# Summing a modulation column two blocks after its load, writing residuals eight products later, and running attention head 0 ahead of delta-rule head 0

## The chip, the cores and the metric

The kernel runs as one program on one core of a Trainium2 chip. The metric is the device time of one execution in microseconds (us); three executions of the kernel before gave a median of 1952.88 us. The core has a matrix engine (TensorE, called PE in the profile; its weight loads are PEld), a vector engine (VectorE, DVE), a scalar engine (ScalarE, ACT), a general engine (GpSimd, POOL), and a sync engine (SyncE, SP), which here issues all DMAs.

## The reference

One decoder layer on 256 rows of width 2048, all in float32:

```
mod = silu(c) @ ada_w + ada_b            # 9 vectors of 2048: sh1 sc1 gt1 sh2 sc2 gt2 sh3 sc3 gt3
h = ada_in(x, norm_g[0], sh1, sc1)       # rmsnorm(x)*(1+scale)+shift
x = x + 0.5 * gt1 * swiglu(h, ...)       # first feed-forward, inner width 5632
h = ada_in(x, norm_g[1], sh2, sc2)
x = x + gt2 * hybrid_mixer(h, ...)       # 8 attention heads with a forget gate (fox), 8 gated delta-rule heads (gdn)
h = ada_in(x, norm_g[2], sh3, sc3)
x = x + 0.5 * gt3 * swiglu(h, ...)       # second feed-forward
return rmsnorm(x, final_norm)
```

## The kernel before, in words

**Products in two parts.** PE multiplies float32 data as a rounded high part plus a low part. Every weight is therefore split on the core. The weights come as 674 blocks of eight 128x128 tiles, in the order in which PE uses them. `Stream.block` issues the DMA of a block on SP (`wraw`, L119) and rounds it on ACT to the high part (`whi`, L121); `Stream.next` subtracts on DVE to get the low part (`wlo`, L133). Each of the three tiles has a pool of four buffers (the raw blocks have one more during the feed-forwards), so SP loads block n when DVE has done `wlo` of block n-4, and DVE can be up to four blocks ahead of PE. In what follows a place is named by block number: blocks 1 to 264 are the first feed-forward, 265 to 378 the mixer's input projections with the heads woven in, 379 to 410 its output projection, 411 to 674 the second feed-forward.

**Modulation columns.** `mod` is computed in 144 columns of 128 values. `ada_col` loads 1 MB of weights for one column (`adat`, L253, on SP right behind a weight load) and then one DVE instruction multiplies and sums it (`total`, L257). The table `RATE` says how many columns are due per block from a given block on (0.1 from block 264, 0.25 from 280, 0.125 from 408). From the mixer on `W.late` is set, and a column's sum is not recorded at its load but put into `W.owing`; the next call of `Stream.next` that opens a block calls `settle`, which records all owed sums. `ada_need`, called before a residual or a norm uses a column, also settles all.

**Mixer.** `ORDER` lists the steps: K, G, V, Z and F project a column group of a head; G starts the delta-rule chain of a head (`gdn`), F the attention chain (`fox`). Chains are generators: between products, `tick` advances a clock by 0.35 per product and lets a chain record its next piece when the number that it yielded has passed. `finish` records all that is left of a chain at once. The chain `solve` inverts 16x16 blocks for four heads: it writes them to DRAM (`ld`, L951), reads them back, does 15 pairs of DVE instructions (L964, L965), writes the result to DRAM (`lt`, L970), reads it back (L974) and multiplies (L977). Step G of head 0 calls `finish("k", 3)`, which needs `solve` of the first four heads.

**Residuals.** After the last product of an output tile, `residual` adds the PSUM tile to `x` with two DVE instructions (L506, L507; L504 before them halves the gate).

**What sets the order.** The code records instructions; the layer that builds the program then orders each engine's queue by the place of recording and by what it estimates to be ready, unless `issue_after` ties an instruction behind another one of its engine. Each engine works through its queue in that order, and an instruction that waits holds up all behind it on that engine.

Of the kernel before, what the change touches and what calls it, by code (L numbers as in the profile page):

```python
# [8 lines left out]
F32 = mybir.dt.float32  # L9
# [4 lines left out]
ALU = mybir.AluOpType  # L14
# [5 lines left out]
KD = D // P  # L20
# [8 lines left out]
WB = 8  # L29
# [3 lines left out]

RATE = ((0, 0.5), (24, 0.34), (56, 0.45), (68, 0.06), (112, 0.5), (168, 0.38), (264, 0.1), (280, 0.25), (408, 0.125))
N_BIG, N_GDN = 3, 3
# [4 lines left out]
HIDX = 3  # L40
MORE = True

HA = 128 + 16
# [4 lines left out]
GAP = {"k": 1.0, "gdn": 1.0, "fox": 1.2, "out": 1.0}  # L48
ORDER = ("K3 K4 K5 K6 K7 Z0 V0 G0 F0 G1 F1 G2 F2 G3 F3 V1 Z1 G4 F4 G5 F5 G6 G7 F6 F7").split()
N_O = 17  # L50
# [38 lines left out]
class Stream:  # L89
# [11 lines left out]

    def settle(self):

        while self.owing:
            self.owing.pop(0)()

# [17 lines left out]
    def next(self, mat, k, n, width=1):  # L124
        i = len(self.order)
        if i % WB == 0:
            nc = self.nc
            b = i // WB
            r, lo = self.first.pop(0) if self.first else self.block(b)
            self.l = lo.tile([P, WB * P], F32R, name="wlo")  # L130
            pace = [r_ for r_ in RATE if r_[0] <= b][-1][1]
            with self.behind():
                nc.vector.tensor_tensor(self.l, r, self.h.bitcast(F32), ALU.subtract)  # L133
            self.settle()
            self.owed += 0.0 if self.quiet else pace
            while self.owed >= 1.0:
                self.owed -= 1.0
                self.side()
# [8 lines left out]
def layer_kernel(ctx: ExitStack, tc: tile.TileContext, xrow, c, adaw, cols, cst, w, out, order, dbg=None):  # L147
# [86 lines left out]
    def ada_col():  # L234
# [20 lines left out]
        def total():  # L255
            with W.behind(False):
                V.tensor_tensor_reduce(t, t, cs, 1.0, L("adab", q, 1), ALU.mult, ALU.add, mod[:, q : q + 1])  # L257
            if (m, j) in ada_done:
                ada_done[m, j]()

        if W.late:
            W.owing.append(total)
        else:
            total()
# [347 lines left out]
    def ffn(which, m_gt, early=None):  # L612
        fs = list(range(NF))
        with tc.tile_pool(name=f"hid{which}", bufs=PARTS[which][1] + HIDX) as hp, \
                tc.tile_pool(name=f"more{which}", bufs=1) as more:
            W.more = more if MORE else None
            for half in range(2):
# [3 lines left out]
                else:  # L621
                    hids = gate_up(which, part, 3 if half == 0 else 1, hp, early if half == 0 else None)
                for j in range(KD):
                    ps = psb("pd")
                    for q, hd in enumerate(hids):
                        mm(ps, W.next(("d", which), part[q], j), hd, q == 0, q == len(part) - 1)
                    residual(ps, j, m_gt, True)
                    if half == 1:
# [8 lines left out]
                        if j == KD // 2:  # L637
                            sqrt_table(x[:, j, :1])
                W.quiet = False
            W.more = None  # L640
# [77 lines left out]
    def mixer():  # L718
# [219 lines left out]
        def solve(half):  # L938
# [24 lines left out]
            for i in range(1, 16):  # L963
                V.tensor_tensor(pv[:, :i, :i], xv[:, :i, :i], bv[:, i, :i].unsqueeze(1).to_broadcast([8 * n, i, i]), ALU.mult)  # L964
                V.tensor_reduce(xv[:, :i, i], pv[:, :i, :i], mybir.AxisListType.X, ALU.add)  # L965
                if i % 3 == 0:
                    yield 1.2
            yield 4.0
            with tc.issue_after(W.last):
# [272 lines left out]


        ko = [NH + h for h in range(4)] + list(range(6)) + [NH + h for h in range(4, NH)] + [6, 7]
        for js in [list(range(4))] + [[j] for j in range(4, KD)]:
# [6 lines left out]
            for i, k in enumerate(ko):  # L1252
                for kind in ("gdn", "out") if k >= NH else ("fox",):
                    finish(kind, k % NH)
                if js[0] == 0 and i == KD - 1:
                    x_back(0)
                for q, j in enumerate(js):
                    mm(pj[q], W.next("o", k, j), oh_[k], i == 0, i == KD - 1)
                    tick(TILE_US)
            for q, j in enumerate(js):  # L1260
                residual(pj[q], j, 5, False)
                sumsq_add(j)
                norm2.y(j)
                if j == KD // 2:
                    sqrt_table(x[:, j, :1])
        mx.close()
# [157 lines left out]
```

## Time and profile before

| what | value |
|---|---|
| median of three executions | 1952.88 us (1949.29 to 1954.36) |
| the profiled execution: its time, its span | 1954.36 us, 1952.6 us |
| PE busy, DVE busy, ACT busy (share of the span) | 97%, 80%, 53% |
| bytes read from HBM, mean rate | 512.89 MB, 265 GB/s |
| granted PE clock, mean | 0.993 |

Busy times are unions of an engine's instructions over the span; the stage windows in the prediction read the same records by stretch. A row of the order of instructions on an engine ends its idle time with a bracket: how long the engine had been idle and which engine's instruction or DMA ended the wait.

### The profile page before, as it was taken

How to read it: one execution, taken by the hardware profiler on the slowest of the kernel's cores; microseconds unless marked ns; L12 is line 12 of the kernel's file. 1: busy time of each engine (PE TensorE's matmuls, PEld its weight loads, DVE VectorE, ACT ScalarE, POOL GpSimd, SP SyncE). 2: the span in 40 equal slices, each digit the busy share in tenths (PEclk: the TensorE clock that was granted, in tenths of full speed). 3: DMA queues.
4: the chain of work that ended last, by engine and by line, in shares of the span. 5: the costliest groups of instructions: out<-in, count | busy, mean ns of one | idle time of the engine just before them, and what ended most of it. 6: DMA issues, size and time to landing. Idle time of an engine off the chain costs nothing.

```text
span 1952.6 us, 33709 instructions
## 1 busy us (share of the span) xinstructions
PE 1902.9 (97%) x13087; PEld 1776.3 (91%) x13087; DVE 1557.3 (80%) x2415; ACT 1035.5 (53%) x1645; POOL 57.0 (3%) x55
## 2 busy tenths in 40 slices
PE   8999999999999999999999999999999999999998
PEld 6999999998999988889989998889999999999997
DVE  6999978989999997889978979886766656565654
ACT  6544554433454446857657655565554445555553
POOL 0000000000000120000000002000000000000011
PEclk8999999999999999999999999999999999999999
DMA  9989867999999986685566658676777665555553
GB/s 369 359 321 349 300 221 254 398 381 376 356 353 342 347 317 218 251 302 205 203 239 236 211 215 315 226 258 249 255 249 239 201 200 203 201 200 202 200 202 119
DMA packets 129490, 519.58 MB, mean 266 GB/s; under 512 B 18217, under 2 KB 21545, under 8 KB 111153
## 3 DMA queue, kind: packets, MB, share of 16 engines
q1 hardware_dynamic: 129330, 517.42, 72.7%
q8 instruction: 103, 1.69, 0.3%
q14 instruction: 57, 0.47, 0.1%
HBM read 512.89 MB, written 4.47 MB: 265 GB/s over the span
## 4 chain that ended last, share of the span: by engine, by line
PE 76%; DVE 11%; DMA 5%; issue 4%; ACT 3%; SPq 0%; DVEq 0%; ACTq 0%
PE pd L482 14%; PE pg L478 10%; PE pu L478 10%; PE pd L483 7%; PE pu L479 5%; PE pg L479 5%; PE pgu L566 5%; PE pgu L565 5%; PE pgu L564 5%; DVE wlo L133 4%; DMA adat<-in_ada_dram 3%; DVE adat L257 2%; PE pp L758 2%; PE pp L759 2%; PE pp L760 2%
## 5 line engine op out<-in xcount | busy, mean ns | idle before, releaser
L133 DVE TENSOR_TENSOR wlo<-wraw,whi 128x1024 fp32r<-128x1024 f32 x674 | 821.1, 1227 | 242.7 <-ACT whi L121 241.3
L121 ACT CAST whi<-wraw 128x1024 fp32r<-128x1024 f32 x674 | 700.1, 1047 | 509.3 <-PE pd L482 166.5
L482 PE MATMUL pd<-hid,whi 128*128 128x512 f32 x1408 | 461.8, 382 | 0.0
L483 PE MATMUL pd<-hid,wlo 128*128 128x256 f32 x1408 | 384.6, 273 | 2.6 <-DVE wlo L133 2.4
L257 DVE CUSTOM_DVE_ANT_0 adat<-adat,cs,colt 128x2048 f32<-128x2048 f32 x140 | 329.5, 2354 | 40.9 <-DMA adat<-in_ada_dram 40.8
L478 PE MATMUL pg<-hs,whi 128*128 128x512 f32 x912 | 302.1, 382 | 2.5 <-DVE shc L429 2.5
L478 PE MATMUL pu<-hs,whi 128*128 128x512 f32 x912 | 302.2, 382 | 0.0
L482 PEld LDWEIGHTS pd<-hid,whi 128*128 128x128 f32 x1408 | 266.0, 189 | 36.5
L483 PEld LDWEIGHTS pd<-hid,wlo 128*128 128x128 f32 x1408 | 270.3, 192 | 5.4 <-DVE wlo L133 5.3
L564 PE MATMUL pgu<-hs,whi 128*128 128x256 f32 x896 | 245.3, 277 | 6.2 <-ACT hs L368 6.2
L479 PE MATMUL pu<-hs,wlo 128*128 128x256 f32 x912 | 249.3, 273 | 0.0
L479 PE MATMUL pg<-hs,wlo 128*128 128x256 f32 x912 | 248.9, 273 | 0.0
L566 PE MATMUL pgu<-hs,wlo 128*128 128x256 f32 x896 | 245.2, 278 | 2.4 <-DVE wlo L133 2.4
L565 PE MATMUL pgu<-hs,whi 128*128 128x256 f32 x896 | 246.8, 277 | 0.0
L478 PEld LDWEIGHTS pg<-hs,whi 128*128 128x128 f32 x912 | 172.4, 189 | 26.7 <-ACT whi L121 2.7
L478 PEld LDWEIGHTS pu<-hs,whi 128*128 128x128 f32 x912 | 172.4, 189 | 23.7
L758 PE MATMUL pp<-hs,whi 128*128 128x256 f32 x656 | 188.9, 289 | 1.5 <-ACT hs L372 1.5
L760 PE MATMUL pp<-hs,wlo 128*128 128x256 f32 x656 | 182.7, 278 | 1.1 <-DVE wlo L133 1.1
L759 PE MATMUL pp<-hs,whi 128*128 128x256 f32 x656 | 182.5, 278 | 0.0
L564 PEld LDWEIGHTS pgu<-hs,whi 128*128 128x128 f32 x896 | 172.3, 193 | 6.9 <-ACT hs L368 6.6
L479 PEld LDWEIGHTS pu<-hs,wlo 128*128 128x128 f32 x912 | 175.0, 192 | 1.3 <-DVE wlo L133 1.2
L479 PEld LDWEIGHTS pg<-hs,wlo 128*128 128x128 f32 x912 | 175.1, 192 | 0.4
(337 smaller groups left out, 2583.6 us busy)
## 6 DMA issues: line engine op xcount, KB each, us to landing
wraw<-in_w_dram SPq DMA_DIRECT2D x674, 512.0 KB, 4.3
adat<-in_ada_dram SPq DMA_DIRECT2D x140, 1024.0 KB, 7.4
xr<-in_xr_dram SPq DMA_DIRECT2D x4, 512.0 KB, 5.1
adaf<-in_ada_dram SPq DMA_DIRECT2D x4, 512.0 KB, 8.7
adaf<-in_ada_dram SPq DMA_DIRECT2D x2, 1024.0 KB, 11.3
xd<-x SPq DMA_DIRECT2D x4, 512.0 KB, 5.0
rw<-rowd SPq DMA_DIRECT2D x16, 128.0 KB, 6.7
x<-xd SPq DMA_DIRECT2D x4, 512.0 KB, 5.4
```

Source lines behind the costliest of these rows:

```text
L121: self.cast = self.nc.scalar.copy(self.h, r).ins
L133: nc.vector.tensor_tensor(self.l, r, self.h.bitcast(F32), ALU.subtract)
L257: V.tensor_tensor_reduce(t, t, cs, 1.0, L("adab", q, 1), ALU.mult, ALU.add, mod[:, q : q + 1])
L478: PE.matmul(ps, wt[0], both, start=(k == 0), stop=False)
L479: PE.matmul(ps[:, T:], wt[1], part(k, HI), start=False, stop=(k == KD - 1))
L482: PE.matmul(ps, wt[0], act.rearrange("p q (a b) -> p q b a", a=2), start=first, stop=False)
L483: PE.matmul(ps[:, :T], wt[1], woven(act[:, 0]), start=False, stop=last)
L564: PE.matmul(o, wh, part(k, HI), start=first and s == 0, stop=False, skip_group_check=skip)
L565: PE.matmul(o, wh, part(k, LO), start=False, stop=False, skip_group_check=skip)
L566: PE.matmul(o, wl, part(k, HI), start=False, stop=last, skip_group_check=skip)
L758: PE.matmul(pp[i][:, :T], wh, hh, start=(k == 0), stop=False)
L760: PE.matmul(pp[i][:, :T], wl, hh, start=False, stop=(k == KD - 1))
```

## The change

Five edits. (1) From the mixer on, an owed sum is recorded with the block it was loaded in, `settle` records only those loaded two or more blocks ago (`BEHIND`), and it ties them behind the `wlo` of the block that has just been opened. (2) `RATE` has no columns from block 264 to 284 and from 404 to 424, and 0.26 per block between. (3) In both feed-forwards and in the output projection, the residual of a tile is recorded after eight products (`LATER`) of the next tile, except for the last tile and for the first group of the output projection. (4) F of heads 0 to 3 stands ahead of G of the same head in `ORDER`. (5) `solve` yields 8.0 instead of 4.0 after its last pair.

```diff
--- before.py
+++ after.py
@@ -31,7 +31,7 @@
 GR = 24
 NEG = -1e30
 
-RATE = ((0, 0.5), (24, 0.34), (56, 0.45), (68, 0.06), (112, 0.5), (168, 0.38), (264, 0.1), (280, 0.25), (408, 0.125))
+RATE = ((0, 0.5), (24, 0.34), (56, 0.45), (68, 0.06), (112, 0.5), (168, 0.38), (264, 0.0), (284, 0.26), (404, 0.0), (424, 0.125))
 N_BIG, N_GDN = 3, 3
 N_FIRST = 4
 AHEAD = 4
@@ -39,6 +39,8 @@
 TILE_US = 0.35
 HIDX = 3
 MORE = True
+LATER = 8
+BEHIND = 2
 
 HA = 128 + 16
 HS = 4 * HA
@@ -46,7 +48,7 @@
 
 BACK = (4, 6, 9)
 GAP = {"k": 1.0, "gdn": 1.0, "fox": 1.2, "out": 1.0}
-ORDER = ("K3 K4 K5 K6 K7 Z0 V0 G0 F0 G1 F1 G2 F2 G3 F3 V1 Z1 G4 F4 G5 F5 G6 G7 F6 F7").split()
+ORDER = ("K3 K4 K5 K6 K7 Z0 V0 F0 G0 F1 G1 F2 G2 F3 G3 V1 Z1 G4 F4 G5 F5 G6 G7 F6 F7").split()
 N_O = 17
 MAGIC = 0x5F3759DF
 
@@ -99,10 +101,10 @@
         self.first = []
         self.late, self.owing = False, []
 
-    def settle(self):
-
-        while self.owing:
-            self.owing.pop(0)()
+    def settle(self, upto=N_TILES):
+
+        while self.owing and self.owing[0][0] <= upto:
+            self.owing.pop(0)[1]()
 
     def behind(self, later=True):
 
@@ -130,8 +132,9 @@
             self.l = lo.tile([P, WB * P], F32R, name="wlo")
             pace = [r_ for r_ in RATE if r_[0] <= b][-1][1]
             with self.behind():
-                nc.vector.tensor_tensor(self.l, r, self.h.bitcast(F32), ALU.subtract)
-            self.settle()
+                lo_ = nc.vector.tensor_tensor(self.l, r, self.h.bitcast(F32), ALU.subtract)
+            with self.tc.issue_after(lo_.ins):
+                self.settle(b - BEHIND)
             self.owed += 0.0 if self.quiet else pace
             while self.owed >= 1.0:
                 self.owed -= 1.0
@@ -253,13 +256,13 @@
                     nc.sync.dma_start(t, adaw[i])
 
         def total():
-            with W.behind(False):
+            with nullcontext() if W.late else W.behind(False):
                 V.tensor_tensor_reduce(t, t, cs, 1.0, L("adab", q, 1), ALU.mult, ALU.add, mod[:, q : q + 1])
             if (m, j) in ada_done:
                 ada_done[m, j]()
 
         if W.late:
-            W.owing.append(total)
+            W.owing.append((len(W.order) // WB, total))
         else:
             total()
 
@@ -620,11 +623,10 @@
                     hids = gate_up_first(part, hp)
                 else:
                     hids = gate_up(which, part, 3 if half == 0 else 1, hp, early if half == 0 else None)
-                for j in range(KD):
-                    ps = psb("pd")
-                    for q, hd in enumerate(hids):
-                        mm(ps, W.next(("d", which), part[q], j), hd, q == 0, q == len(part) - 1)
-                    residual(ps, j, m_gt, True)
+                pds = {}
+
+                def after(j):
+                    residual(pds.pop(j), j, m_gt, True)
                     if half == 1:
                         sumsq_add(j)
                         if which == 1:
@@ -636,6 +638,15 @@
                             W.quiet = True
                         if j == KD // 2:
                             sqrt_table(x[:, j, :1])
+
+                for j in range(KD):
+                    ps = psb("pd")
+                    for q, hd in enumerate(hids):
+                        if j and q == LATER:
+                            after(j - 1)
+                        mm(ps, W.next(("d", which), part[q], j), hd, q == 0, q == len(part) - 1)
+                    pds[j] = ps
+                after(KD - 1)
                 W.quiet = False
             W.more = None
 
@@ -965,7 +976,7 @@
                 V.tensor_reduce(xv[:, :i, i], pv[:, :i, :i], mybir.AxisListType.X, ALU.add)
                 if i % 3 == 0:
                     yield 1.2
-            yield 4.0
+            yield 8.0
             with tc.issue_after(W.last):
                 nc.sync.dma_start(lt[ht].rearrange("n b e -> (n b) e"), xt_)
             yield 3.0
@@ -1241,6 +1252,7 @@
             step(name[0], int(name[1]))
 
 
+        owed = []
         ko = [NH + h for h in range(4)] + list(range(6)) + [NH + h for h in range(4, NH)] + [6, 7]
         for js in [list(range(4))] + [[j] for j in range(4, KD)]:
 
@@ -1254,15 +1266,24 @@
                     finish(kind, k % NH)
                 if js[0] == 0 and i == KD - 1:
                     x_back(0)
+                if owed and i == LATER:
+                    owed.pop(0)()
                 for q, j in enumerate(js):
                     mm(pj[q], W.next("o", k, j), oh_[k], i == 0, i == KD - 1)
                     tick(TILE_US)
-            for q, j in enumerate(js):
-                residual(pj[q], j, 5, False)
-                sumsq_add(j)
-                norm2.y(j)
-                if j == KD // 2:
-                    sqrt_table(x[:, j, :1])
+
+            def after(js=js, pj=pj):
+                for q, j in enumerate(js):
+                    residual(pj[q], j, 5, False)
+                    sumsq_add(j)
+                    norm2.y(j)
+                    if j == KD // 2:
+                        sqrt_table(x[:, j, :1])
+
+            if j == 3 or j == KD - 1:
+                after()
+            else:
+                owed.append(after)
         mx.close()
 
     if dbg is None or "mix" in dbg:
```

The following rows are read from the programs of the two kernels, in queue order. Numbers in names tell buffers apart; line numbers after the change are two to eleven higher.

**Where the sum of a column stands against its load.** The first two pieces are SP's queue before and after the change, near block 360 (heads 5 and 6): `wraw` loads a weight block, `adat` a column.

```order
L119 DMA wraw_12247<-in_w_dram 128x1024
L119 DMA wraw_12301<-in_w_dram 128x1024
L119 DMA wraw_12338<-in_w_dram 128x1024
L119 DMA wraw_12408<-in_w_dram 128x1024
L253 DMA adat_12414<-in_ada_dram 128x2048
```

```order
L121 DMA wraw_12242<-in_w_dram 128x1024
L256 DMA adat_12248<-in_ada_dram 128x2048
L121 DMA wraw_12297<-in_w_dram 128x1024
L121 DMA wraw_12334<-in_w_dram 128x1024
L121 DMA wraw_12405<-in_w_dram 128x1024
```

The same column now loads behind block 359 instead of block 362. DVE's queue at the same place follows, before and after; `wlo` marks the blocks, L257 and L260 are the sum, `st` and `vz` are steps of delta-rule head 5.

```order
L133 TENSOR_TENSOR wlo_12251<-wraw_12247,whi_12249 128x1024
L1149 TENSOR_SCALAR fmx_12071<-fmx_12071 128x2
L1098 COPY st_12093<-pst_12091 128x128
L1137 TENSOR_TENSOR fm_12494<-fm_12494,cstt_88 128x384
L1090 TENSOR_TENSOR vz_8270<-u_12057,po_12061 64x128
L1169 SCALAR_TENSOR_TENSOR fzz_12072<-fzz_12072 128x2
L257 ISA adat_12414,mod_126<-adat_12414,cs_86,colt_87 128x2048
L257 ISA mod_126 128x1
L1100 SCALAR_TENSOR_TENSOR st_12131<-st_12093,rw_11052,pst_12129 128x128
```

```order
L135 TENSOR_TENSOR wlo_12338<-wraw_12334,whi_12336 128x1024
L289 TENSOR_TENSOR rsa_f_12163<-rsy_f_12162 128x2
L1101 TENSOR_TENSOR vz_8270<-u_12051,po_12055 64x128
L290 SCALAR_TENSOR_TENSOR rsa_f_12163<-rsa_f_12163,fss_12155 128x2
L260 ISA adat_12248,mod_126<-adat_12248,cs_86,colt_87 128x2048
L260 ISA mod_126 128x1
```

Before, the sum stood behind `wlo` of block 359, three blocks ahead of the block its load follows; now it stands behind `wlo` of block 361, two blocks past it. All 24 columns loaded behind blocks 286 to 375 are now summed two blocks past their load; before, 23 columns loaded in that stretch were summed zero to three blocks ahead of it.

**Where the solved blocks go through DRAM.** SP's queue before and after, behind the value projection V of heads 0 to 3 (blocks 302 to 306): `lt` is written from `x` and read back.

```order
L119 DMA wraw_9572<-in_w_dram 128x1024
L970 DMA lt_8240<-x_85 64x256
L253 DMA adat_9578<-in_ada_dram 128x2048
L974 DMA x_85<-lt_8240 128x8x16
L859 DMA rw_9635<-rowd_8234 128x256
L119 DMA wraw_9638<-in_w_dram 128x1024
```

```order
L121 DMA wraw_9603<-in_w_dram 128x1024
L981 DMA lt_8240<-x_85 64x256
L121 DMA wraw_9647<-in_w_dram 128x1024
L121 DMA wraw_9688<-in_w_dram 128x1024
L985 DMA x_85<-lt_8240 128x8x16
L121 DMA wraw_9765<-in_w_dram 128x1024
```

Write, column load, read-back and row fetch stood together between blocks 302 and 303; now the write stands behind block 303 and the read-back behind block 305.

**The end of the output projection.** DVE's queue before and after, from block 409 on: two residuals and the next norm's input `hs`.

```order
L133 TENSOR_TENSOR wlo_14298<-wraw_14294,whi_14296 128x1024
L506 SCALAR_TENSOR_TENSOR x_85<-po_14182,mod_126,x_85 128x256
L257 ISA adat_14372,mod_126<-adat_14372,cs_86,colt_87 128x2048
L257 ISA mod_126 128x1
L507 SCALAR_TENSOR_TENSOR x_85<-po_14182,mod_126,x_85 128x256
L133 TENSOR_TENSOR wlo_14320<-wraw_14316,whi_14318 128x1024
```

```order
L135 TENSOR_TENSOR wlo_14283<-wraw_14279,whi_14281 128x1024
L509 SCALAR_TENSOR_TENSOR x_85<-po_14170,mod_126,x_85 128x256
L510 SCALAR_TENSOR_TENSOR x_85<-po_14170,mod_126,x_85 128x256
L135 TENSOR_TENSOR wlo_14314<-wraw_14310,whi_14312 128x1024
L409 SCALAR_TENSOR_TENSOR hs_127<-x_85,g1_14252,hs_127 128x2x128
```

The sum between the two residual instructions is gone: no column is loaded behind blocks 404 to 426. In the two feed-forwards, the DVE queue keeps every residual behind the same block as before but for one instruction in the second, which stands a block earlier; in the first feed-forward the queues of PE and DVE are row for row those of before.

## Prediction

> **What bounds the kernel now.** I read the page's busy times and the shares of the chain that ended last first, then a table of stages, then the waits inside the stages that the change touches.
>
> ```profile
> span 1952.6 us, 33709 instructions
> PE 1902.9 (97%) x13087; PEld 1776.3 (91%) x13087; DVE 1557.3 (80%) x2415; ACT 1035.5 (53%) x1645; POOL 57.0 (3%) x55
> PE 76%; DVE 11%; DMA 5%; issue 4%; ACT 3%; SPq 0%; DVEq 0%; ACTq 0%
> ```
>
> PE is the bound, and no product is removed, so what can be won is PE's idle time: 1952.6 - 1902.9 = 49.7 us. The stages say where it lies. Columns: stretch and its length, then busy time (instructions) of PE, PEld, DVE, ACT and POOL, granted PE clock, DMA share, GB/s.
>
> ```profile
> 400.00:725.00 325.00, 322.70 (x1953) 293.92 (x1952) 299.68 (x352) 150.02 (x200) 18.71 (x11) 1.00 0.93 354
> 775.00:875.00 100.00, 95.17 (x655) 87.79 (x654) 87.02 (x183) 73.11 (x143) 0.43 (x2) 1.00 0.76 273
> 875.00:1000.00 125.00, 119.25 (x957) 113.57 (x956) 110.90 (x323) 82.59 (x200) 0.00 (x0) 1.00 0.58 202
> 1000.00:1175.00 175.00, 170.81 (x1309) 161.99 (x1309) 142.92 (x318) 106.73 (x223) 0.00 (x0) 1.00 0.64 234
> 1175.00:1300.00 125.00, 118.38 (x813) 110.64 (x812) 115.73 (x188) 75.52 (x123) 14.98 (x14) 1.00 0.73 262
> 1300.00:1925.00 625.00, 625.00 (x3817) 574.52 (x3816) 398.58 (x505) 309.57 (x425) 15.94 (x12) 1.00 0.63 217
> ```
>
> The program's queues first differ in the mixer, about 770 us in. From 775 to 1300 us (mixer, output projection, start of the second feed-forward) PE is idle for 4.83 + 5.75 + 4.19 + 6.62 = 21.4 us; from 1300 to 1925 not at all. So 21.4 us is all that the change can win. DVE is busy 87 to 93% in three of those four rows: it is the second bound, and DVE's own waits are dear there.
>
> ```profile
> L133 DVE TENSOR_TENSOR wlo<-wraw,whi 128x1024 fp32r<-128x1024 f32 x158 | 193.1, 1225 | 25.2 <-ACT whi L121 24.4 <-PE pp L758 0.2
> L257 DVE CUSTOM_DVE_ANT_0 adat<-adat,cs,colt 128x2048 f32<-128x2048 f32 x35 | 82.6, 2359 | 14.1 <-DMA adat<-in_ada_dram 14.0
> L257 DVE CUSTOM_DVE_ANT_0 adat<-adat,cs,colt 128x2048 f32<-128x2048 f32 x10 | 23.5, 2351 | 24.1 <-DMA adat<-in_ada_dram 24.1
> ```
>
> These are groups by line: the first two of 775 to 1300 us, the third of 1300 to 1925 us. In the first window 158 blocks pass, one in 525 / 158 = 3.3 us; 35 sums take 2.36 us each and DVE stands 14.0 us before them waiting for the load. The DMA issues by line give the load's median time from issue to landing (the last figure):
>
> ```profile
> adat<-in_ada_dram SPq DMA_DIRECT2D x140, 1024.0 KB, 7.4
> ```
>
> In the second feed-forward the same wait is 24.1 us, and PE is busy 625.00 of 625: there it is covered.
>
> **Part 1: sums two blocks past the load.** Where a sum waits and PE stops soon after, pairs of rows from the timelines of DVE and PE show it (the bracket is idle time and what ended it), with two DMA pieces of the chain.
>
> ```profile
> 941.71 2.35 DVE L257 CUSTOM_DVE_ANT_0 adat<-adat,cs,colt 128x2048 f32<-128x2048 f32 x1 [0.72 <-DMA adat<-in_ada_dram]
> 945.54 0.63 PE L1061 MATMUL pn<-Z,Tm 128*128 128x64 f32 x4 [0.63 <-DVE Z L1018]
> 987.67 2.35 DVE L257 CUSTOM_DVE_ANT_0 adat<-adat,cs,colt 128x2048 f32<-128x2048 f32 x1 [2.05 <-DMA adat<-in_ada_dram]
> 990.35 0.49 PE L1089 MATMUL po<-st,wq 128*128 128x128 f32 x2 [1.07 <-DVE st L1100]
> 993.01 0.49 PE L1092 MATMUL po<-vz,At 128*128 128x128 f32 x2 [0.88 <-DVE vz L1090]
> 1054.57 7.61 DMA adat<-in_ada_dram
> 1062.20 2.35 DVE L257 CUSTOM_DVE_ANT_0 adat<-adat,cs,colt 128x2048 f32<-128x2048 f32 x1 [2.69 <-DMA adat<-in_ada_dram]
> 1064.88 0.49 PE L1089 MATMUL po<-st,wq 128*128 128x128 f32 x2 [1.91 <-DVE st L1100]
> 1227.61 7.92 DMA adat<-in_ada_dram
> 1235.55 2.35 DVE L257 CUSTOM_DVE_ANT_0 adat<-adat,cs,colt 128x2048 f32<-128x2048 f32 x1 [2.52 <-DMA adat<-in_ada_dram]
> 1239.49 0.38 PE L483 MATMUL po<-oh,wlo 128*128 128x256 f32 x1 [2.38 <-DVE wlo L133]
> 1254.62 2.35 DVE L257 CUSTOM_DVE_ANT_0 adat<-adat,cs,colt 128x2048 f32<-128x2048 f32 x1 [2.60 <-DMA adat<-in_ada_dram]
> 1260.88 0.38 PE L423 MATMUL pg<-hs,wlo 128*128 128x258 f32 x1 [0.35 <-DVE wlo L133]
> ```
>
> The load that ends at 1062.18 was issued at 1054.57, and one `wlo` stood between it and its sum on DVE. Queued behind that waiting sum is `st`, for which PE stood 1.91 us. Over the five places PE loses 0.63 + 1.07 + 0.88 + 1.91 + 2.38 + 0.35 = 7.2 us. After the change a load is issued when `wlo` of four blocks earlier is done, and its sum stands two blocks later than the load: six `wlo` lie between. Alone they take 6 x 1.225 = 7.4 us, and at the block pace above 20 us; a load takes 7.6 to 7.9. So the first three places (4.5 us) should go, and the last two (2.7 us) go because no column is loaded behind blocks 404 to 426. The ends are 0 (another wait takes each place) and 7.2; I take 7.2, since 20 us is far over 7.9. The output projection is not covered by the two-block rule: each residual settles everything owed, so its five sums stand one or two blocks ahead of the block their load follows, much as before; their waits can stay, and I count no gain for them. The later sum keeps its buffer longer: the next load but one comes eight blocks on, issued four `wlo` past this load's block, when the sum (two past) is done. Nothing waits.
>
> **Part 2: fewer columns at the edges.** From block 272 to 424 31 columns are loaded instead of 35. The four sums (9.4 us of DVE) move into the second feed-forward, where PE covered ten of them with their waits; DVE has 625 - 398.6 us to spare there. Price 0; if the cover went, each could cost up to its 2.35 us. One more place is freed, since no sum stands behind blocks 389 to 393 any more (DVE's chain, then PE):
>
> ```profile
> 1183.15 2.26 DVE adat L257
> 1187.07 0.38 PE L483 MATMUL po<-oh,wlo 128*128 128x256 f32 x1 [0.80 <-DVE wlo L133]
> ```
>
> Gain 0.8 us.
>
> **Part 3: attention head 0 first, and a longer last yield in `solve`.** Before, step G of head 0 forced all of `solve` at its end. The rows are SP's, ACT's and PE's.
>
> ```profile
> 846.58 0.46 SPq L970 DMA_DIRECT2D lt<-x  x1
> 849.62 1.76 SPq L119 DMA_DIRECT2D wraw<-in_w_dram  x3
> 857.15 1.05 ACT L121 CAST whi<-wraw 128x1024 fp32r<-128x1024 f32 x1 [7.90 <-DMA wraw<-in_w_dram]
> 859.51 0.38 PE L760 MATMUL pp<-hs,wlo 128*128 128x256 f32 x1 [0.77 <-DVE wlo L133]
> 862.83 0.38 PE L760 MATMUL pp<-hs,wlo 128*128 128x256 f32 x1 [0.38 <-DVE wlo L133]
> 870.03 0.33 PE L1004 MATMUL pvq<-colt,qv 128*128 128x128 f32 x1 [2.53 <-ACT kk L930]
> 871.47 0.71 PE L1008 MATMUL pkq<-qv,kk 128*128 128x128 f32 x4 [0.34 <-DVE Ln L936]
> ```
>
> SP held the next weight loads behind `lt` and its read-back until 849.62, ACT got its block at 857.15 after 7.90 us, DVE and PE followed, and ACT then worked off its backlog late. PE lost 0.77 + 0.38 + 2.53 + 0.34 = 4.0 us. Now F of head 0 gives the chain four more blocks, some 13 us; `lt` waits for the 15th pair, which stands behind `wlo` 300, and the weight load behind it needs `wlo` 300 anyway. Moved on SP with it are eight `ld` writes, the read-back and row fetches of about 0.4 us each to issue, past weight loads that wait for DVE anyway. I take 4.0; the lower bound is 1.15 (the two `wlo` waits alone). The yield also moves the second `lt` three blocks later, two blocks ahead of V of heads 4 to 7, which forces it: 0 to 4.0 lost there again, and I take 0, since the read-back (`lt` to `x`) still stands before that step.
>
> Moving F moves everything in the heads, and the order shows two more table loads on ACT:
>
> ```profile
> L911 ACT ACT_TABLE_LOAD x11 | 14.1, 1283 | 3.0 <-DVE rsy_f L282 2.4 <-DVE cv L910 0.4
> 972.87 2.35 DVE L257 CUSTOM_DVE_ANT_0 adat<-adat,cs,colt 128x2048 f32<-128x2048 f32 x1 [0.27 <-DMA adat<-in_ada_dram]
> 975.58 0.38 PE L1053 MATMUL put<-colt,U 128*64 128x128 f32 x2 [1.06 <-DVE U L1043]
> ```
>
> Two loads are 2.6 us of ACT, which is busy 66 to 73% where the heads begin. The last row is one of the short hand-off waits that make up the other 21.4 - 12.0 = 9.4 us (7.2, 0.8 and 4.0 being named). Rearranged hand-offs can cost from -9.4 (all go, as DVE has 14.0 + 9.4 us less to do or wait) to +9.4 (they double). I take +2.5, near the table loads, because other pieces pile up anew.
>
> **Part 4: residuals eight products later.** In the feed-forwards the queues hardly differ (one DVE instruction in the second), so the 2.3 us of PE idle from 400 to 725 us stay: 0. In the output projection residuals come up to one block earlier on DVE: at most the longest stop of that stretch, 2.38 us, either way; 0 taken, since `wlo` keeps its place.
>
> **Sum.** -7.2 - 0.8 - 4.0 + 2.5 = -9.5 us. The profiled execution took 1954.36 us, 1.5 above the median of 1952.88; against the median this gives 1943.4 us.
>
> [...]
>
> **Rivals.**
> 1. The likeliest: named waits go, little comes back, 1943.4 us, its own range 1939 to 1947. Chance 0.55.
> 2. DVE's freed 23 us take most of the unnamed hand-offs too: -12.0 - 7 = 1934 to 1939. For: DVE is at 87 to 93%. Against: the consumers still stand about two blocks behind their producers. Chance 0.16.
> 3. The wait only passes on: the next hand-off in the head's chain stops PE instead of the one removed, so of 12.0 us only the two places at the end of the output projection and part 2 stay, 3.5 us, less 2.5: 1947 to 1955, no change. For: after 972.87, with 0.27 us of waiting only, PE still stood 1.06. Chance 0.13.
> 4. The load is hidden anyway: had the load of 1227.61 landed by 1233.03 (1235.55 less 2.52, when DVE came to it), 5.4 us after its issue, the places of part 1 would owe their stops to the sums' own 2.35 us, which stay. Then -0.8 - 4.0 + 2.5 gives 1950.6 us. Against: the median load takes 7.4 us. Chance 0.05.
> 5. Slower: a sum tied right behind a `wlo` stands in front of a chain's step at every place. Price 1.06 us, the row at 975.58, whose `U` came behind a sum of 2.35 us. At all 24 pinned sums it is 25.4 us, less 12.0: 1966 us. It decides from (12.0 + 5.9) / 1.06 = 17 of 24 on. Against: before, sums stood behind a `wlo` mostly too, and PE stood after few. Chance 0.11.
>
> **Numbers.** 0.3% is 5.9 us, about what a measurement of this kernel tells from no change. Faster: cases 1 and 2, 0.71; the same: cases 3 and 4, 0.18; slower: case 5, 0.11. The range leaves out case 5 and the far end of case 2: 1935 to 1955.
>
> **What would show it.** Right: DVE's wait for `adat` from 775 to 1300 us falls from 14.0 to under 4 us, with 31 sums there; no idle of 7.90 on ACT near 857; PE idle from 775 to 1300 us near 12 us; nothing new before 775 or after 1300. Wrong: PE waits behind sums at `st`, `vz`, `U` as often as before, with no DMA wait in front; a stop at V of heads 4 to 7; or gaps in the second feed-forward where its 14 sums wait.

## The result, and the profile after

The changed kernel takes 1941.66 us (median of four executions, 1940.34 to 1943.79), the kernel before 1952.54 beside it: ratio 0.9948, 95% interval 0.9935 to 0.9961, that is 7.6 to 12.7 us faster. The forecast was 1943.4. The profiled execution took 1943.79 us, 10.6 less than the profiled one of before.

The head of the page of the changed kernel: its span, the busy times, and the chain of work that ended last.

```profile
span 1941.9 us, 33701 instructions
PE 1903.0 (98%) x13087; PEld 1777.2 (92%) x13087; DVE 1554.0 (80%) x2415; ACT 1041.2 (54%) x1647; POOL 56.8 (3%) x55
PE 37%; DVE 2%; issue 1%; ACT 0%; DMA 0%; SPq 0%; DVEq 0%; ACTq 0%
```

PE's busy time is what it was, so the time came out of its idle time. The chain covers only 40% of the span this time and is not used further. The stages, in the columns of the prediction's table:

```profile
400.00:725.00 325.00, 322.69 (x1953) 293.89 (x1951) 299.90 (x351) 150.20 (x200) 18.70 (x11) 1.00 0.92 352
775.00:875.00 100.00, 95.99 (x653) 88.83 (x653) 77.43 (x167) 69.04 (x129) 0.42 (x2) 0.98 0.73 257
875.00:1000.00 125.00, 121.87 (x970) 116.19 (x969) 117.34 (x329) 87.99 (x207) 0.00 (x0) 1.00 0.64 222
1000.00:1175.00 175.00, 172.05 (x1329) 163.28 (x1329) 147.20 (x337) 111.45 (x236) 0.00 (x0) 1.00 0.65 237
1175.00:1300.00 125.00, 123.70 (x845) 115.31 (x844) 111.14 (x180) 79.31 (x128) 14.78 (x14) 1.00 0.69 247
1300.00:1925.00 625.00, 625.00 (x3819) 574.76 (x3818) 406.16 (x513) 309.51 (x423) 18.09 (x14) 1.00 0.63 219
```

From 775 to 1300 us PE's idle time falls from 21.4 to 4.01 + 3.13 + 2.95 + 1.30 = 11.4 us; in the first and the last row nothing moves. The row of 775 to 875 us also has a granted clock of 0.98, where it had been 1.00: 1.7 us of PE's speed, of which more below. Over the whole span PE's idle time goes from 1952.6 - 1902.9 = 49.7 to 1941.9 - 1903.0 = 38.9 us, which is 10.8 less: 10.0 in this stretch, and 0.8 in the first 100 us (88.14 us busy before, 88.96 after), where the change moves nothing. The 1.7 us at half clock are part of PE's busy time, which came out as before nevertheless; what makes up for them is in no row that I can name.

DVE's groups by line, the first two of 775 to 1300 us, the third of 1300 to 1925 us:

```profile
L135 DVE TENSOR_TENSOR wlo<-wraw,whi 128x1024 fp32r<-128x1024 f32 x162 | 197.4, 1219 | 38.3 <-ACT whi L123 37.8
L260 DVE CUSTOM_DVE_ANT_0 adat<-adat,cs,colt 128x2048 f32<-128x2048 f32 x32 | 75.0, 2344 | 0.8 <-DMA adat<-in_ada_dram 0.8
L260 DVE CUSTOM_DVE_ANT_0 adat<-adat,cs,colt 128x2048 f32<-128x2048 f32 x14 | 32.9, 2347 | 4.1 <-DMA adat<-in_ada_dram 4.1
```

The sums' wait for their loads is gone (14.0 to 0.8 us, and 24.1 to 4.1 where it was covered). DVE now idles in front of `wlo` instead (25.2 to 38.3 us), waiting for ACT: it has caught up with ACT. PE, which stood 4.7 us for `wlo` in this stretch before, stands 0.7 us for it now.

What PE still stops for, from its timeline, with the instruction on ACT that makes the first stop (`fm` is the first step of attention head 0 and reads `rw`, a row fetched from DRAM; `kk` are keys of a delta-rule head; the time of a row is when the stop ends):

```profile
803.72 0.40 ACT L1147 ACTIVATE fm<-rw,colS 128x128 f32<-128x128 f32 x1 [2.30 <-DMA rw<-rowd]
810.42 0.71 PE L937 MATMUL pkk<-kk 128*128 128x128 f32 x4 [2.73 <-ACT kk L941]
869.89 0.33 PE L1167 MATMUL ppt<-colt,x 128*128 128x128 f32 x1 [1.11 <-ACT x L1162]
884.65 0.30 PE L1189 MATMUL pft<-colt,on 128*128 128x128 f32 x1 [1.45 <-issue]
1268.83 0.46 PE L481 MATMUL pg<-hs,whi 128*128 128x512 f32 x1 [0.49 <-DVE shc L432]
```

The stop at 810.42 was 0.55 us before. The one of 2.53 us at 870.03 is gone; those at 869.89 and 884.65 stand before other products, of the attention chain, and are new. The last row is the start of the second feed-forward, where PE's timeline of the kernel before has this, which the prediction had not named:

```profile
1279.54 0.45 PE L478 MATMUL pg<-hs,whi 128*128 128x512 f32 x1 [2.53 <-DVE shc L429]
```

### The profile page after: what moved, and what is told of

The parts are those of the page before. It is cut to its first block, busy times and chain, and to the rows that moved or that the text cites. A ratio compares the mean times of both kernels' runs of the same rounds, so it can differ in the third digit from the quotient of the medians.

```text
span 1941.9 us, 33701 instructions
## 1 busy us (share of the span) xinstructions
PE 1903.0 (98%) x13087; PEld 1777.2 (92%) x13087; DVE 1554.0 (80%) x2415; ACT 1041.2 (54%) x1647; POOL 56.8 (3%) x55
## 5 line engine op out<-in xcount | busy, mean ns | idle before, releaser
L260 DVE CUSTOM_DVE_ANT_0 adat<-adat,cs,colt 128x2048 f32<-128x2048 f32 x140 | 329.2, 2351 | 6.5 <-DMA adat<-in_ada_dram 6.5
```

## The experiments

The theory: a sum that waits for its load on DVE holds the small hand-offs behind it, PE stands for them, and the pin takes the wait away. The rivals: the wait only passes on; the pinned sums stand before chain steps; or it is another part that gains. Four kernels have one part alone on the kernel before, four lack one part of the changed kernel, and the last ones split parts 1 and 3. The ratios are to executions of the kernel before beside each run, with medians of 1951.3 us for the four parts alone, 1951.9 for the four that lack a part and 1950.4 for the last ones; so between groups a ratio is a safer measure than a median. One row of PE, DVE and clock over 775 to 1300 us serves as the measure inside a trace; this is the one of before.

```profile
775.00:1300.00 525.00, 503.60 (x3729) 473.98 (x3729) 456.57 (x1009) 337.95 (x688) 15.41 (x16) 1.00 0.67 241
```

### Part 1 alone

```diff
-            self.settle()
+            with self.tc.issue_after(lo_.ins):
+                self.settle(b - BEHIND)
```

> Only part 1 on the kernel before: the sum stands two blocks past its load and right behind that block's wlo; all 35 columns stay, G comes before F, residuals stay. Theory A (what PE lost behind waiting sums is won): the three places in the heads go, 0.63 + 1.07 + 0.88 + 1.91 = 4.5 us; the two places at the end of the output projection and the stop at the start of the second feed-forward stay, since each residual there settles all sums owed: 1948.0 us against 1952.5. Theory B (the wait only passes on to the next hand-off): 1951.5 to 1953.5 us, though DVE's wait for adat falls. Theory C (a pinned sum stands before chain steps): above 1953.5 us.

Measured: 1947.11 us against 1951.3, ratio 0.9977 (0.9967 to 0.9986). The stretch as a window row:

```profile
775.00:1300.00 525.00, 510.46 (x3778) 481.69 (x3777) 460.22 (x1017) 344.58 (x696) 15.57 (x16) 1.00 0.69 245
```

DVE's sums in it, from the groups by line:

```profile
L259 DVE CUSTOM_DVE_ANT_0 adat<-adat,cs,colt 128x2048 f32<-128x2048 f32 x36 | 84.9, 2357 | 0.0
```

And, from PE's timeline, the one stop that has a drop of the clock behind it:

```profile
1240.90 0.61 PE L322 MATMUL nsum<-colt,sq 128*128 128x2 f32 x4 [1.60 <-ACT sq L308]
```

The wait is gone to the last tenth with 36 sums in place, and PE is idle for 14.5 instead of 21.4 us. Of these 6.9 us, 1.7 are lost to a lower clock after the stop of 1.60 (granted 0.60 and 0.55 over 1242 to 1244 and 1244 to 1246 us). The time fits theory A (4.2 us for 4.5) and not theory B. But the stop of 2.38 us at the end of the output projection went too, though the columns behind the last blocks are still loaded: the prediction had given that one to part 2. In its place two others of that stage grew, the norm's from 0.56 to the 1.60 above, and the 0.80 us at 1187.07 to this:

```profile
1182.49 0.38 PE L485 MATMUL po<-oh,wlo 128*128 128x256 f32 x1 [1.74 <-DVE wlo L134]
```

So from 1175 to 1300 us PE's idle time fell from 6.62 to 4.57 us only: there, part of the wait did pass on.

### Part 2 alone

```diff
-RATE = (..., (264, 0.1), (280, 0.25), (408, 0.125))
+RATE = (..., (264, 0.0), (284, 0.26), (404, 0.0), (424, 0.125))
```

> Only part 2 on the kernel before: 31 columns instead of 35 from block 272 to 424, none behind the first and last blocks of that stretch. Theory A: the two places at the end of the output projection (2.38 + 0.35 us), the one of 0.80 us before them and the stop of 2.53 us at the start of the second feed-forward, of which the trace after still shows 0.49, go: 2.7 + 0.8 + 2.0 = 5.5 us, 1947.0 against 1952.5. As the prediction had it, without the last of these, 3.5 us: 1949.0. Theory B (the four sums cost what they cost wherever they stand): 1952.5, with new stops of PE in the second feed-forward.

Measured: 1949.33 us, ratio 0.9990 (0.9981 to 0.9999): some 2 us, less than either sum. The stop at the start of the second feed-forward fell from 2.53 to 0.49 us, with one of 1.03 for `hs` some 11 us behind it; those of 2.38 and 0.80 became 0.88 and 0.70 at other blocks; and the one of 2.53 us at 870.03, before `pvq`, grew to 3.96, with a drop of the clock behind it (0.69 over 870 to 875 us). DVE's waits for loads stayed (16.5 us).

### Part 4 alone

```diff
                     for q, hd in enumerate(hids):
+                        if j and q == LATER:
+                            after(j - 1)
...
+                if owed and i == LATER:
+                    owed.pop(0)()
```

> Only part 4 on the kernel before: residuals written eight products into the next tile. Theory A (wlo sets the pace, residuals do not): 1952.5 us within 1. Theory B (the residuals were what held wlo in the output projection): faster by up to 2.4 us, 1950.1, with the stop of 2.38 us at block 404 or so gone.

Measured: 1961.96 us, ratio 1.0049 (1.0037 to 1.0062): 7 to 12 us slower, which neither theory had. The trace shows two pairs of a waiting sum and a stop of PE (DVE's row, then PE's, from their timelines):

```profile
1038.62 2.35 DVE L258 CUSTOM_DVE_ANT_0 adat<-adat,cs,colt 128x2048 f32<-128x2048 f32 x1 [3.08 <-DMA adat<-in_ada_dram]
1044.03 1.09 PE L1050 MATMUL pn<-Z,Tm 128*128 128x64 f32 x4 [2.94 <-DVE Z L1027]
1245.45 2.35 DVE L258 CUSTOM_DVE_ANT_0 adat<-adat,cs,colt 128x2048 f32<-128x2048 f32 x1 [1.53 <-DMA adat<-in_ada_dram]
1248.77 1.01 PE L321 MATMUL nsum<-colt,sq 128*128 128x2 f32 x4 [3.91 <-ACT sq L307]
```

The windows about the second pair, in which the third column from the end is the granted clock:

```profile
1240.00:1244.00 4.00, 4.00 (x37) 3.97 (x36) 3.92 (x5) 3.52 (x5) 1.07 (x1) 1.00 0.90 328
1244.00:1248.00 4.00, 0.85 (x9) 0.77 (x7) 2.55 (x3) 0.20 (x1) 0.00 (x0) 0.99 0.87 328
1248.00:1252.00 4.00, 3.23 (x15) 3.23 (x16) 3.86 (x11) 1.10 (x3) 0.00 (x0) 0.50 0.40 134
1252.00:1256.00 4.00, 4.00 (x26) 4.00 (x26) 1.34 (x2) 1.05 (x1) 0.00 (x0) 0.65 0.52 152
```

A sum now stood between the two instructions of the last residual: its wait and its own 2.35 us held `sq`, the norm, and PE for 3.91 us, and then PE ran at half clock. With a stop of 3.48 us at 873.17 there are three stops with a drop behind them; (1 - clock) summed over windows of 5 us gives 8.6 us lost to the clock. PE's idle time is not longer than before, 525 - 505.70 = 19.3 us:

```profile
775.00:1300.00 525.00, 505.70 (x3713) 477.65 (x3713) 458.18 (x1007) 339.32 (x686) 16.80 (x16) 0.98 0.68 241
```

In the second feed-forward, too, PE stopped for 1.86 us (at 1490.52) behind a sum that had waited 3.03 us, so what the prediction called covered there is not covered in every order.

Why do sums move at all, and in the heads, which part 4 does not touch? The layer that orders the queues decides anew: in the program as built, 422 of the 12822 products and weight loads in PE's queue are not those that stood at the same place before, and all of them lie between the heads and the start of the second feed-forward. An edit in one place can shift waits in other places where sums are not tied.

### Part 3 alone

```diff
-... Z0 V0 G0 F0 G1 F1 G2 F2 G3 F3 V1 ...
+... Z0 V0 F0 G0 F1 G1 F2 G2 F3 G3 V1 ...
-            yield 4.0
+            yield 8.0
```

> Only part 3 on the kernel before: F of heads 0 to 3 before G, and the longer last yield of solve. Theory A: the stops of 0.77 + 0.38 + 2.53 + 0.34 = 4.0 us from 858 to 871 us go, and new stops come (in the trace after, 2.73 instead of 0.55 us at 807 and 1.11 us at 868, 3.3 in all): 1951.8 us against 1952.5; by the prediction's 2.5 for new stops 1951.0. Theory B (the new stop at 807 needs the pinned sums too): 1948.5. Theory C (without the pin the sums, which wait, meet the moved steps worse): above 1953.5.

Measured: 1949.72 us, ratio 0.9994 (0.9985 to 1.0003), no difference that can be told. The stops from 858 to 871 us are gone, but a new one of 3.04 us stands before a product of the attention chain (`ppt`, at 869.90), and the clock dropped twice (0.66 over 870 to 875 us, 0.50 over 1274 to 1276; 3.4 us lost), the second time after the stop at the second feed-forward's start, 2.46 us here. The stop at 810 us, 2.73 in the changed kernel, is 0.56 here; it is not the pin that it needs, as theory B had it, since the run without part 1 below has it at 1.86.

### Without part 1

The diff is the one of part 1 alone, taken back.

> The changed kernel without part 1: sums again at the next block, tied to an earlier instruction only; 31 columns, F first, residuals later stay. If the parts add up, it is slower than the changed kernel by what part 1 alone won, 4.2 us: 1945.9 against 1941.7. If they do not (part 4 moves the waiting sums to worse places, as it did alone, where 9 to 10 us were lost, 7 of them by the granted clock after stops of 2.9 and 3.9 us), about as slow as the kernel before or slower, 1950 to 1956, with PE stops near or above 2.7 us in the heads and a granted clock under 1.00 after them. DVE's wait for adat from 775 to 1300 us: back to 9 to 16 us either way.

Measured: 1948.43 us, ratio 0.9987 (0.9976 to 0.9997): 6.8 us slower than the changed kernel by the medians. The sums' group by line:

```profile
L258 DVE CUSTOM_DVE_ANT_0 adat<-adat,cs,colt 128x2048 f32<-128x2048 f32 x33 | 77.4, 2345 | 13.9 <-DMA adat<-in_ada_dram 13.9
```

One waiting sum and the stop behind it, from the timelines of DVE and PE:

```profile
1005.43 2.35 DVE L258 CUSTOM_DVE_ANT_0 adat<-adat,cs,colt 128x2048 f32<-128x2048 f32 x1 [2.82 <-DMA adat<-in_ada_dram]
1008.23 0.49 PE L1098 MATMUL po<-st,wq 128*128 128x128 f32 x2 [2.04 <-DVE st L1109]
```

The window row:

```profile
775.00:1300.00 525.00, 508.27 (x3747) 480.09 (x3747) 450.25 (x1002) 343.90 (x691) 17.12 (x16) 0.99 0.68 236
```

The 13.9 us are back, and with them a sum, `st` and PE in the very chain that the prediction read from the trace of before. Idle time is 16.7 us, the clock costs 5.2 (it is 0.50 over 809 to 811 us, 0.70 over 870 to 875 and 0.51 over 1011 to 1013). The two intervals lie apart. By the medians part 1 carries about six tenths of the gain, by the ratios (0.0039 of 0.0052) three quarters.

### Without part 2

```diff
-RATE = (..., (264, 0.0), (284, 0.26), (404, 0.0), (424, 0.125))
+RATE = (..., (264, 0.1), (280, 0.25), (408, 0.125))
```

> The changed kernel without part 2: 35 columns from block 272 to 424, the last ones behind the end of the output projection. If the parts add up: 2.0 us slower, 1943.7. If part 2 is what keeps a sum from standing in front of the last residuals (in the run of part 4 alone a sum there made PE stop 3.91 us at the norm and run at half clock for some 6 us): 5 to 8 us slower, 1947 to 1950, with a stop of over 2.7 us near 1240 and the clock under 1.00 behind it.

Measured: 1943.46 us, ratio 0.9963 (0.9951 to 0.9975): 1.8 us slower than the changed kernel by the medians, as if the parts added up; but the two intervals overlap, and this run alone does not show a gain of part 2. No stop came at the norm, since with the pin the sums hardly wait (0.6 us in all). PE's idle time in the stretch is 11.8 us against 11.4, with one drop of the clock in each. The stop at 810 us is 0.53 us here, but one of 2.13 for `wlo` stands at 869.40, with the drop behind it (0.50 over 871 to 873 us), and the start of the second feed-forward costs 1.71 us instead of 0.49:

```profile
869.40 0.38 PE L771 MATMUL pp<-hs,wlo 128*128 128x256 f32 x1 [2.13 <-DVE wlo L135]
1270.02 0.46 PE L481 MATMUL pg<-hs,whi 128*128 128x512 f32 x1 [1.71 <-DVE shc L432]
```

### Without part 4

The diff is the one of part 4, taken back.

> The changed kernel without part 4. If the parts add up, part 4 costs 10 us here too and this is at 1932. If part 4 only hurts where a waiting sum stands among the residuals, of which parts 1 and 2 leave none: within 2 us of 1941.7.

Measured: 1945.99 us (1942.45 to 1947.61), ratio 0.9971 (0.9959 to 0.9982). Its interval meets that of the second measurement of the changed kernel below (0.9940 to 0.9973), so whether part 4 wins anything beside the others stays open; that it costs 10 us there is excluded. The profiled execution was the fastest of six, 1942.45 us, and shows no clock drop and 12.6 us of idle time; it says nothing of where the slower five lose theirs.

### Without part 3

The diff is the one of part 3, taken back.

> The changed kernel without part 3: G before F, the short last yield. By the prediction's terms: 4.0 - 2.5 = 1.5 us slower, 1943.2; if the parts add up 1.6 slower. If the stop of 2.73 us at 807 us and the half clock after it (1.7 us) come from part 3 alone, they go with it, 4.4 - 0.5 us, and the 4.0 us of stops from 858 to 871 come back as far as pinned sums leave them (3.0 us in the run of part 1 alone, there without a drop of the clock): within 2 us of 1941.7, with a stop near 868 instead of one at 807.

Measured: 1938.82 us (1936.74 to 1940.76), ratio 0.9936 (0.9924 to 0.9948): 2.8 us faster than the changed kernel by the medians, though the two intervals meet. The window row:

```profile
775.00:1300.00 525.00, 516.95 (x3828) 487.96 (x3827) 458.77 (x1015) 349.01 (x702) 15.21 (x16) 1.00 0.69 242
```

And PE's timeline, where the changed kernel stops at 810 and 870 us:

```profile
808.99 0.71 PE L937 MATMUL pkk<-kk 128*128 128x128 f32 x4 [0.33 <-ACT kk L941]
869.33 0.33 PE L1015 MATMUL pvq<-colt,qv 128*128 128x128 f32 x1 [0.76 <-ACT qv L922]
```

Of the 4.0 us of stops that part 3 was to take away, one of over half a microsecond is left without it, of 0.76: here the other parts had done it. ACT's idle of 7.90 us near 857, on which part 3's term was built, is gone too (2.15 at most from 840 to 872 us). Idle time is 8.0 us against 11.4, and the clock never drops.

### The changed kernel once more

No edit; it stands beside the three that follow.

> The changed kernel itself once more, beside the three that follow: 1941.7 us, ratio 0.9948. [...]

Measured: 1942.03 us (1941.32 to 1945.70), ratio 0.9957 (0.9940 to 0.9973). The stop at 810 us came again, 2.08 us long, and the clock did not drop. For comparison, the windows about the stop in the changed kernel's first profile:

```profile
807.00:811.00 4.00, 1.26 (x10) 0.93 (x9) 0.69 (x4) 3.98 (x12) 0.00 (x0) 1.00 0.20 82
811.00:815.00 4.00, 4.00 (x13) 3.19 (x12) 3.80 (x10) 4.00 (x11) 0.00 (x0) 0.58 0.31 91
815.00:819.00 4.00, 4.00 (x23) 3.53 (x22) 2.79 (x6) 2.63 (x8) 0.00 (x0) 1.00 1.01 403
```

The stop's row from PE's timeline of this run, and then its windows:

```profile
809.29 0.71 PE L937 MATMUL pkk<-kk 128*128 128x128 f32 x4 [2.08 <-ACT kk L941]
```

```profile
809.00:813.00 4.00, 3.71 (x19) 3.33 (x20) 3.62 (x11) 4.00 (x11) 0.00 (x0) 1.00 0.06 11
813.00:817.00 4.00, 4.00 (x24) 3.52 (x23) 4.00 (x8) 4.00 (x10) 0.00 (x0) 1.00 0.98 391
```

In the window with the drop, 811 to 815, PE counts as busy for 4.00 of 4 us and does 13 products, where it does 19 to 24 in the later windows shown: here the busy time hides the clock.

### G first again, the longer yield kept

```diff
-... Z0 V0 F0 G0 F1 G1 F2 G2 F3 G3 V1 ...
+... Z0 V0 G0 F0 G1 F1 G2 F2 G3 F3 V1 ...
```

> The changed kernel with G ahead of F again for heads 0 to 3, the longer last yield kept. Theory A (F first is what costs: it puts the fm activations, which wait for rowd, in front of kk on ACT): as the kernel without part 3, 1938 to 1939, 3 us faster than the changed kernel, no stop over 1 us near 807. Theory B (the yield is what costs, it moves the second solve's hand-offs): 1941 to 1942. Theory C (the longer yield is what kept the stops of 858 to 871 us away): slower than without part 3, 1940 or more, with stops over 1 us near 868.

Measured: 1939.61 us (1938.15 to 1941.40), ratio 0.9938 (0.9923 to 0.9953), 2.4 us under the changed kernel beside it; of the six executions only the slowest, 1941.40, is above the fastest of the changed kernel, 1941.32. So it is the order of the heads that costs, not the yield. Of theory C it has the stop near 868 (2.24 us), which the kernel without all of part 3 had at 0.76, at no price that the medians can tell.

### The fm activations later

```diff
             for t, o, wd in ((0, 0, P), (1, P, T)):
+              with tc.issue_after(W.cast) if h == 0 else nullcontext():
                 A.activation(fm[:, o : o + wd], cb[:, :wd], AF.Identity, bias=colS[:, t, 0, h : h + 1], scale=-1.0)
```

> The changed kernel with one thing more: the three fm activations of head 0's F may not be issued before the latest whi cast at that point, so on ACT they stand some 15 casts later, behind kk. Theory A (the 2.30 us that ACT waits for rowd at fm are what stops PE at 807 us): the stop of 2.73 us falls under 1, the clock stays at 1.00 there, 2 + 1.7 us faster than the changed kernel: 1938. Theory B (kk is late for another reason, the table load and eight Ln exponentials ahead of it): the stop stays, 1941 to 1942.

Measured: 1939.71 us (1937.92 to 1940.47), ratio 0.9938 (0.9922 to 0.9954): 2.3 us under the changed kernel, and all five executions are below all six of it. PE's wait at the same product, from its timeline:

```profile
808.99 0.71 PE L937 MATMUL pkk<-kk 128*128 128x128 f32 x4 [0.34 <-ACT kk L941]
```

The window row:

```profile
775.00:1300.00 525.00, 516.30 (x3822) 486.37 (x3821) 457.09 (x1014) 349.52 (x703) 15.20 (x16) 1.00 0.68 242
```

The stop is gone with F still first, though the table load (1.28 us) and the eight exponentials (2.45 us) still stand ahead of `kk`: the cause was one activation that waited for a DMA in front of them. Other runs with F first bear it out, since `fm` waits for a different time in each. ACT's row and PE's row from the run without part 4, the one without part 1, and the one with the sums one block past their load (next section):

```profile
800.45 0.40 ACT L1138 ACTIVATE fm<-rw,colS 128x128 f32<-128x128 f32 x1 [0.38 <-DMA rw<-rowd]
807.16 0.71 PE L928 MATMUL pkk<-kk 128*128 128x128 f32 x4 [0.81 <-ACT kk L932]
801.09 0.40 ACT L1145 ACTIVATE fm<-rw,colS 128x128 f32<-128x128 f32 x1 [1.43 <-DMA rw<-rowd]
807.79 0.92 PE L935 MATMUL pkk<-kk 128*128 128x128 f32 x4 [1.86 <-ACT kk L939]
804.70 0.40 ACT L1147 ACTIVATE fm<-rw,colS 128x128 f32<-128x128 f32 x1 [2.42 <-DMA rw<-rowd]
811.40 0.71 PE L937 MATMUL pkk<-kk 128*128 128x128 f32 x4 [2.85 <-ACT kk L941]
```

Each stop is the wait of `fm` plus 0.43 us, as are the changed kernel's 2.73 (wait 2.30) and, measured again, 2.08 (wait 1.65). Where `fm` does not wait (without part 2) or stands behind `kk` (part 3 alone), the stop is 0.53 and 0.56. So F first costs here only where the row fetch is late; why it is later in some runs than in others is not shown.

### Pinned one block past the load

```diff
-BEHIND = 2
+BEHIND = 1
```

> The changed kernel with the sums pinned one block past their load instead of two. Five wlo then lie between the issue of a load and its sum, 16.5 us at the pace of 3.3 us a block, against a load of 7.4 to 7.9 us. Theory A (the pin alone does it, since unpinned sums drift to before the load's own block): DVE's wait for adat stays under 2 us and the time within 2 us of the changed kernel. Theory B (the second block is needed because blocks bunch up, two wlo following each other at 1.2 us): wait for adat 3 us or more, 2 to 4 us slower.

Measured: 1941.29 us (1939.89 to 1943.68), ratio 0.9949 (0.9934 to 0.9964), the same as the changed kernel. The sums of 775 to 1300 us, from the groups by line:

```profile
L260 DVE CUSTOM_DVE_ANT_0 adat<-adat,cs,colt 128x2048 f32<-128x2048 f32 x33 | 77.3, 2344 | 0.0
```

One block is enough. In the order of the program with two blocks and no tie, the sums of the heads stand zero to three blocks ahead of the block their load follows, as in the kernel before; that one was not run. Together they suggest that the tie does the work, and not the number of blocks.

## Why the prediction was right, and where it was not

**The time** was right: -9.5 us was forecast from 1954.36, and the profiled execution lost 10.6. PE's idle time from 775 to 1300 us came to 11.4 where 12 was said, DVE's wait to 0.8 where under 4 was said, and there is no gap in the second feed-forward. The terms are another matter. That their sum came out so close is in part luck: part 3 was off by some 4 us (-1.5 forecast, about +2.4 measured beside the others), and what made up for it stood in no term: the 2.0 us at the start of the second feed-forward, and what part 4 may win beside the others.

**Part 1** (-7.2). The mechanism is shown from three sides: alone it takes all waits for loads away and wins 4.2 us, without it 13.9 us of waits are back and 6.8 us are lost, and the same chain of sum, `st` and PE is there again. The split was wrong: the stops of 2.7 us at the end of the output projection, which "go because no column is loaded behind blocks 404 to 426", go by the pin alone too, though with part 1 alone two other stops of that stage grow by 2.0 us. Six `wlo` were counted as cover; five do.

**Part 2** (-0.8). Measured -2.0 alone and, not clear of noise, -1.8 on top of the others. Over half of that was missing: the stop at the start of the second feed-forward, 2.53 us before and 0.49 after, which is 1.71 without part 2, stood in the trace of before and was in no term.

**Part 3** (-4.0 + 2.5). Wrong in sign. Alone it makes no difference that can be told, and beside the others its order of the heads costs about 2.4 us. Two steps failed. "I take 4.0" counted stops that parts 1, 2 and 4 leave at 0.76 without it (at 2.24 where the longer yield stays), so there was little left to win. And "I take +2.5" for rearranged hand-offs was too low for this place: the stop at 810 is 2.18 us more than before, those at 870 and 884 are new with 1.11 and 1.45, 4.7 us together, and the half clock, in one of its two profiles, is 1.7. (Elsewhere short hand-offs shrank, which is why the idle time came out as said.) The place was in the text only as two table loads; what held PE at 810 was `fm`, waiting for a row fetch on ACT's queue. The stop at 884 is still there with `fm` later (1.44 us); its cause stays open. A moved step was costed by what it issues, not by what its first instruction waits for.

**Part 4** (0, at most 2.38 either way). Taken back from the changed kernel it costs 4.3 us by the medians, which is not clear of noise; alone it is 7 to 12 us slower, far outside the bound. The bound was the longest stop of the stretch, and it left out that the order elsewhere changes, that a sum can fall between the two instructions of the last residual, and the 8.6 us that the lower clock cost after three stops.

**The parts do not add up**: -4.2 - 2.0 + 10.7 - 1.6 = +2.9 us by the medians, against -10.9 together. The traces fit a simple reason: once sums are tied and wait 0.8 us in all, the moved residuals have nothing to collide with.

**The rivals.** That the wait passes on (3) is excluded as the rule by part 1 alone (idle time 6.9 us less); at the end of the output projection part of it did. That loads are hidden anyway (4) is excluded by the 13.9 us without part 1. Chain steps behind pinned sums (5) are not seen: in part 1 alone PE's idle time fell by 6.9 us with all sums pinned. That most of the unnamed hand-offs go as well (2) did not happen in the changed kernel; without part 3 idle time is 8.0 us and the time 1938.8, inside that rival's 1934 to 1939.

## What to carry to other kernels

On an engine that works through its queue in order, look for the instruction that waits for a DMA and ask which small hand-offs stand behind it (without part 1 a sum on DVE waited 2.82 us for its load, and PE stood 2.04 us for the `st` behind it); tie it behind work that certainly covers the transfer, rather than trust the place where it was written. When a step is moved forward, cost its first wait as well as its instructions: what was hidden at the old place (here a row fetch, 2.30 us) may stand in front of the critical hand-off at the new one. Try parts of a change alone and each taken back: one of the four here only harmed on its own, and the kernel without another has the lowest median of all.

## What the runs showed of the hardware

In some of these runs a drop of the granted clock followed a stop of PE, so that the stop cost more than itself. After the one at 810.42 us in the changed kernel's first profile, the granted clock, read in windows of 0.5 us, is 0.62 from 811.5, 0.50 in the six from 812 to 815, and 0.97 from 815: 0.50 for some 3.4 us, which is 1.7 us of work (0.58 over the window of 4 us from 811 above: 0.42 x 4 = 1.7); after the stops of 2.94 and 3.91 us in part 4 alone it lasted about twice as long (0.50 and 0.65 over two windows of 4 us: 2.0 + 1.4). The length of the stop alone does not tell in these runs whether a drop follows. From 775 us on, stops of 1.60 (part 1 alone), 1.86 and 2.04 (without part 1), 2.13 (without part 2) and 2.46 us (part 3 alone) had the drop behind them, stops of 2.53 (before, twice), 2.38 (before), 2.29 (without part 4), 2.24 (G first again) and 1.86 us (part 4 alone, second feed-forward) had not, and the same stop of the changed kernel had it at 2.73 and not at 2.08. All from 2.59 us up (eight of them) had it. What sets such stops apart no run here shows.
